# The last norm of a decoder step: sums of squares on TensorE block by block, the three column groups in another order, the last scaling on VectorE alone

## The chip, the core and the metric

The kernel runs on one core of a Trainium2 chip. The metric is the device time of one execution in microseconds. The profile shows one execution, with the engines PE (TensorE matmuls), PEld (TensorE weight loads), DVE (VectorE), ACT (ScalarE), POOL (GpSimd) and the DMA queues of SP and ACT.

## The reference

One layer of a hybrid autoregressive decoder is applied to 1024 prompt tokens and to 64 sampled tokens (8 sequences of 8). Each token has 1024 values. A token-mixing sub-layer (short convolution, dilated attention, sliding-window attention) and a SwiGLU feed-forward sub-layer add to the residual stream, each with its own modulated RMSNorm. At the end comes a plain RMSNorm, and it is this part that the change touches:

```
def rmsnorm(x, g):
    x32 = x.astype(jnp.float32)
    y = x32 * lax.rsqrt(jnp.mean(x32 * x32, axis=-1, keepdims=True) + EPS)
    return (y * g.astype(jnp.float32)).astype(x.dtype)

def swiglu(h, w_gate_up, w_down):
    gate, up = jnp.split(h @ w_gate_up, 2, axis=-1)
    return (jax.nn.silu(gate) * up) @ w_down
...
    x = x + gate2 * swiglu(rmsnorm(x, g_ffn) * (1 + scale2) + shift2, w_gate_up, w_down)
...
    y_prompt = rmsnorm(y_p, norm_final)
    y_sample = rmsnorm(y_s, norm_final)
```

## The kernel before

Everything is held transposed: a token is a column, its 1024 values lie in 8 blocks of 128 partitions. The residual stream is `x1[0]` to `x1[7]`, each 128 x 1088 in float32, columns 0 to 1023 the prompt and 1024 to 1087 the sampled tokens. All large matmuls are made in three passes (lines 204 to 206, `mm3`): weights and activations are each split into a high and a low half, and high x high, high x low and low x high are added up in PSUM. PSUM has eight banks, given out under four tags: `g` three, `s` two, `t` two, `o` one.

The feed-forward hidden values are made in groups of two blocks of 128 (`FF_GROUPS`); each group's down projection is added to the residual stream. For all groups but the last this goes by `down_all`. For the last group the columns are cut in three by `LAST`, so that the final norm of one group of columns can go on beside the down projection of the next. The last hidden block is split into its halves in three column parts (`split_hid`, lines 852 and 853): columns 366 to 731 first, 0 to 365 next, 732 to 1087 last.

For one group of n columns the code before does this:

1. For each of the 8 blocks m, `down` (line 1063): six matmuls of n columns into a bank with tag `g`, then `add_gated` on VectorE: bank times gate plus `x1[m]` (line 764), and for the sampled tokens two more short operations (768, 769).
2. `rstd` (line 1064): ScalarE squares each `x1[k]` (791, 794); seven adds gather the squares in `lacc` (795), on VectorE or GpSimd as `FADD` says; then, for each tile of 128 columns, a matmul with `lacc` as the stationary operand and a column of ones sums over the partitions (798). In the trace each tile shows as two passes.
3. `inv_rms` (lines 233 to 239): six short operations on VectorE and a square root on ScalarE give one scale per token.
4. The scale is spread over all partitions by matmuls with the identity (802) into a bank with tag `s`.
5. The scaling: for the blocks in `FPOOL` ScalarE multiplies with the gain (1071) and GpSimd with the scale (1072), which ScalarE has copied out of PSUM (1067); for the others VectorE does both in one operation (1074). Each block then goes out by its own DMA (1075), issued in turn by ScalarE and SyncE.

The program is written with a tile framework that orders each engine's instructions when it is built: it plays the program through with modelled durations and lets an engine take, of the instructions that are ready, the one that stands first in the code. So work that stands later in the code can be drawn ahead, but the engine then runs the order fixed at build time and waits wherever the chip is late. The pool `fin` takes the memory of the pool `sums`, whose last reader is a matmul of the last hidden block.

Of the kernel before, what the change touches and what calls it, by code (L numbers as in the profile page):

```python
# [8 lines left out]
F32 = mybir.dt.float32  # L9
F32R = mybir.dt.float32r  # L10
AF = mybir.ActivationFunctionType
OP = mybir.AluOpType
# [3 lines left out]
KC = 8  # L16
# [10 lines left out]
GRP = ((0, 366), (366, 366), (732, 356))  # L27
NB = 10
CONV_B = ((0,), (), (1,))
LAST = ((0, 416), (416, 416), (832, 256))  # L30
FF_GROUPS = ((0, 4), (20, 2)) + tuple((f, 2) for f in range(4, 20, 2))


# [12 lines left out]
ACCE = tuple("vvvvvggv")  # L46
MIXE = tuple("vgvgvgvg")
NADD = tuple("gggvgggv")
FADD = (tuple("ggvggvgv"), tuple("vgggvgvg"), tuple("vvvvvvvv"))
FPOOL = ((2, 3, 4), (1, 2, 3, 4, 5), (2, 4, 7))  # L50

MODN = (2, 1, 1, 0, 1, 0, 1, 1, 2, 1, 2, 0)
NPRE = 2
# [2 lines left out]
def build(nc, tc, d):  # L56
    st = tc.tile_pool
    with st(name="const", bufs=1) as cst, st(name="rows", bufs=1) as rows, \
            st(name="act", bufs=1) as actp, st(name="stream", bufs=1) as stream, \
            st(name="psum", bufs=1, space=PSUM) as psum:  # L60
        _build(nc, tc, d, cst, rows, actp, stream, psum)


def _build(nc, tc, d, cst, rows, actp, stream, psum):
    V, S, G, PE, SP = nc.vector, nc.scalar, nc.gpsimd, nc.tensor, nc.sync
# [3 lines left out]
    start = ExitStack()  # L69
    stp = start.enter_context(tc.tile_pool(name="start", bufs=1))  # L70

    def eng(c):
        return G if c == "g" else V

    def ps_tile(tag):
        bufs = {"g": PSB[0], "s": PSB[1], "t": PSB[2], "o": PSB[3]}[tag]
        return psum.tile([128, 512], F32, tag=tag, bufs=bufs, name="ps_" + tag)

    def row(name):
        return rows.tile([128, T], F32, tag="row", bufs=ROWS, name=name)  # L80
# [55 lines left out]
    gT = cst.tile([128, 24], F32, name="gT")  # L136
# [7 lines left out]
    ones = cst.tile([128, 1], F32, name="ones")  # L144
# [67 lines left out]
    def asel(acts, g):  # L212
        n = GRP[g][1] + (state["nb"] if acts is h and g == 2 else 0)
        return n, lambda h, k: acts[g][:, h, k, :n]
# [13 lines left out]
    def inv_rms(pool, sums, n):  # L228

        v = pool.tile([128, n], F32, tag="ir_v", bufs=2, name="ir_v")  # L230
        y = pool.tile([128, n], F32, tag="ir_y", bufs=2, name="ir_y")
        t = pool.tile([128, n], F32, tag="ir_t", bufs=2, name="ir_t")
        V.tensor_scalar(v, sums, 1.0 / D, EPS, op0=OP.mult, op1=OP.add)
        S.activation(y, v, AF.Sqrt)
        V.reciprocal(y, y)
        V.tensor_mul(t, y, y)
        V.tensor_mul(t, t, v)
        V.tensor_scalar(t, t, -0.5, 1.5, op0=OP.mult, op1=OP.add)
        V.tensor_mul(y, y, t)
        return y  # L240
# [11 lines left out]
    for item in "m0 w0 m1 x0 x1 m2 x2 m3 x3 x4 w1 x5 x7 x6 m4 m5 m6 m7".split():  # L252
        kind, i = item[0], int(item[1:])
# [37 lines left out]
    for k in range(KC):  # L291
        if k % 2 == 0:
            mod_tile(k // 2, bank="o" if k % 4 else "t")
        r, s = xr[k], MOD[:, 8 + k, 0:1]
        ts = stp.tile([128, NS], F32, tag="tsx", bufs=2, name="tsx")
        V.tensor_tensor(bi(ts), bi(r[:, SEQ:]), modb(8 + k), op=OP.mult)
        for g, (c0, n) in enumerate(GRP):
            m = min(n, SEQ - c0)
            S.activation(h[g][:, 0, k, :m], r[:, c0:c0 + m], AF.Copy, scale=s)
            V.scalar_tensor_tensor(h[g][:, 1, k, :m], r[:, c0:c0 + m], s, h[g][:, 0, k, :m].bitcast(F32),  # L300
                                   op0=OP.mult, op1=OP.subtract)
# [3 lines left out]
        for b in range(2):  # L305
            for g in range(3):
                n, a = asel(h, g)
# [68 lines left out]
    for i, (name, scale) in enumerate(early):  # L376
        r = prow[name] = row("p_" + name)
# [9 lines left out]
    c0 = GRP[2][1]  # L387
# [4 lines left out]
    for i, (name, scale) in enumerate(early):  # L392
        ps = ps_tile(SHB[i % 4])
        first = None
        for hf in range(2):
            for q in (3, 2, 1, 0):
                with tc.issue_after(first.ins) if first is not None else ExitStack():
                    ins = PE.matmul(ps[32 * q:32 * q + 32, :128], lhsT=shT[:, hf * 4 + q, :],
                                    rhs=wraw[i, hf][:, q * 128:q * 128 + 128], start=(hf == 0), stop=(hf == 1))
# [209 lines left out]
    mx, x1 = {}, {}  # L609
# [25 lines left out]
    ps = ps_tile("t")  # L635
# [138 lines left out]
    def tmp():  # L774
        if "ff" in scratch:
            return scratch["ff"].tile([128, 416], F32, tag="tmp", bufs=3, name="tmp")
        scratch["i"] = i = (scratch.get("i", 0) + 1) % 13
        return scratch["free"][:, 768 + 366 * i:768 + 366 * (i + 1)]
# [6 lines left out]
    def rstd(rng, adds, acc):  # L785

        c0, n = rng
        nt = (n + 127) // 128
        if n < nt * 128:
            G.memset(acc[:, n:nt * 128], 1.0)  # L790
        S.activation(acc[:, :n], x1[0][:, c0:c0 + n], AF.Square)
        for k in range(1, KC):
            sq = tmp()
            S.activation(sq[:, :n], x1[k][:, c0:c0 + n], AF.Square)
            eng(adds[k]).tensor_add(acc[:, :n], acc[:, :n], sq[:, :n])
        ps = ps_tile("t" if "ff" in scratch else "g")
        for t in range(nt):
            PE.matmul(ps[:, t:t + 1], lhsT=acc[:, t * 128:(t + 1) * 128], rhs=ones, start=True, stop=True)
        y = inv_rms(cst, ps[:, :nt], nt)
        r = ps_tile("s" if "ff" in scratch else "g")  # L800
        for t in range(nt):
            PE.matmul(r[:, t * 128:(t + 1) * 128], lhsT=y[:, t:t + 1].to_broadcast([128, 128]), rhs=ident,
                      start=True, stop=True)
        return r
# [3 lines left out]
    def second_rstd(g):  # L808
        return rstd(GRP[g], NADD, acc_tile(g))
# [45 lines left out]
    def down(w, m, rng, hid):  # L855
        c0, n = rng
        ps = ps_tile("g")
        mm3(ps, w, [(k, k) for k in range(len(hid))], lambda hl, k: hid[k][:, hl, c0:c0 + n], n)
        add_gated(m, rng, ps, 40)
# [69 lines left out]
    with tc.tile_pool(name="ffn", bufs=1, reuse_waits="tile") as ff:  # L929
# [96 lines left out]
        for f0, nf in FF_GROUPS[:1]:  # L1026
# [8 lines left out]
            for m in range(KC):  # L1035
                ps = ps_tile("g")
# [17 lines left out]
        fin = sums.enter_context(tc.tile_pool(name="fin", bufs=1, reuse_waits="tile"))  # L1054
# [3 lines left out]
        for q in range(4):  # L1058
            w = wsel(split(d["w_d2"][f0 // 2 - 2, q]))
            ws += [lambda hl, k, w=w, x=x: w(hl, 2 * x + k) for x in range(2)]  # L1060
        for g, (c0, n) in enumerate(LAST):
            for m in range(KC):
                down(ws[m], m, (c0, n), hid)
            r = rstd((c0, n), FADD[g], fin.tile([128, 512], F32, tag="lacc", bufs=1, name="lacc"))
            if FPOOL[g]:
                rs = fin.tile([128, 416], F32, tag="rs", bufs=1, name="rs")
                S.activation(rs[:, :n], r[:, :n], AF.Copy)
            for k in range(KC):
                y, gain = x1[k][:, c0:c0 + n], gT[:, 16 + k:17 + k]
                if k in FPOOL[g]:  # L1070
                    S.activation(y, y, AF.Copy, scale=gain)
                    G.tensor_tensor(y, y, rs[:, :n], op=OP.mult)
                else:
                    V.scalar_tensor_tensor(y, y, gain, r[:, :n], op0=OP.mult, op1=OP.mult)
                (SP if k % 2 else S).dma_start(d["yT"][k][:, c0:c0 + n], y)
        sums.close()
    assert not state["copies"]

# [140 lines left out]
```

## Time and profile before

| | us |
|---|---|
| median of 3 runs | 1404.19 |
| lowest and highest run | 1402.57, 1410.77 |
| the profiled execution | 1407.32 |
| its span in the profile | 1405.5 |
| mean granted clock of TensorE | 0.981 of full |
| VectorE busy | 839.7 |
| ScalarE busy | 582.6 |
| GpSimd busy | 329.6 |

The profiled execution was 1407.32 us by the device's time; its trace covers 1405.5 us of that. A row of the order of time gives the start, the duration, the engine, the line, the operation, what it writes and reads, and how often (xN) it stands in a row; in brackets is the time that the engine was idle before it, and whom it waited for. A row of a group gives the count, the busy time in us and the mean in ns of one, then the idle time before them. Matmuls overlap: the distance from one start to the next is what one costs in a stream, not its duration. A row of a table by stretch gives its bounds, its length, the busy time of each engine with the number of instructions, the granted clock, the share of the DMA engines and GB/s.

### The profile page before, as it was taken

The page shows a single profiled execution, that of the slowest core. Times are in us where ns is not written, and L with a number is a line of the kernel's source. Part 1 is how long each engine was busy: PE and PEld are TensorE (multiplying, and loading weights), DVE is VectorE, ACT ScalarE, POOL GpSimd, SP SyncE. Part 2 cuts the span into 40 slices and gives each one's busy share as a digit, 9 for nine tenths or more (in the row PEclk, how much of TensorE's full clock was granted, in tenths as well). Part 3 has the DMA queues.
Part 4 walks back from the last instruction along what each step waited for, and adds up shares of the span by engine and source line. Part 5 has one row for each costly group of instructions (what it writes and reads, how often), then busy time and mean ns, then how long its engine had stood idle before and what let it go on. Part 6 is the DMA issues. An engine that isn't in the chain of part 4 may idle for free.

```text
span 1405.5 us, 23915 instructions
## 1 busy us (share of the span) xinstructions
PE 1353.1 (96%) x9097; PEld 1288.3 (92%) x9097; DVE 839.7 (60%) x1935; ACT 582.6 (41%) x1204; POOL 329.6 (23%) x364
## 2 busy tenths in 40 slices
PE   7999999999999998899998999999999999999995
PEld 5889999988898887798998999999999999999994
DVE  5467768255676326224569675757565666665656
ACT  5397764365654335132345413141313232322243
POOL 2143343233424230102124020202111111111114
PEclk9999999999999999999999999999999999999996
DMA  9342431352416669675443413151515142323103
GB/s 356 113 160 99 135 99 24 129 197 91 144 24 218 216 240 362 239 284 174 112 134 93 143 38 120 30 180 31 188 30 187 51 160 81 137 83 128 44 30 128
DMA packets 77188, 190.91 MB, mean 136 GB/s; under 512 B 14048, under 2 KB 23808, under 8 KB 76288
## 3 DMA queue, kind: packets, MB, share of 16 engines
q1 hardware_dynamic: 73376, 135.67, 29.5%
q10 hardware_dynamic: 3536, 53.65, 10.6%
q8 instruction: 72, 1.18, 0.3%
q14 instruction: 44, 0.36, 0.1%
q0 software_dynamic: 160, 0.04, 0.0%
HBM read 181.32 MB, written 59.33 MB: 171 GB/s over the span
## 4 chain that ended last, share of the span: by engine, by line
PE 86%; DVE 6%; DMA 4%; issue 2%; ACT 1%; POOL 1%; POOLq 0%; SPq 0%; ACTq 0%; DVEq 0%
PE ps_g L204 19%; PE ps_g L205 19%; PE ps_g L206 19%; PE ps_s L205 3%; PE ps_s L204 3%; PE ps_s L206 3%; PE ps_o L578 2%; PE ps_t L205 2%; PE ps_t L204 2%; PE ps_t L206 2%; PE ps_t L569 2%; DMA wraw<-in_w_gu 1%; PE ps_g L179 1%; PE ps_s L527 1%; PE ps_s L528 1%
## 5 line engine op out<-in xcount | busy, mean ns | idle before, releaser
L204 PE MATMUL ps_g<-act,wsp 128*128 128x366 f32 (+1 forms) x1192 | 400.1, 337 | 2.6 <-DVE u L327 2.6
L206 PE MATMUL ps_g<-act,wsp 128*128 128x366 f32 (+1 forms) x1192 | 395.9, 333 | 4.0 <-DVE wsp L91 4.0
L205 PE MATMUL ps_g<-act,wsp 128*128 128x366 f32 (+1 forms) x1192 | 398.0, 334 | 0.5 <-DVE act L616 0.5
L90 ACT ACTIVATE wsp<-wraw 128x512 fp32r<-128x512 f32 x232 | 145.4, 629 | 278.1 <-PE ps_g L206 170.1
L204 PEld LDWEIGHTS ps_g<-act,wsp 128*128 128x128 f32 x1192 | 227.5, 191 | 9.9 <-issue 6.1
L206 PEld LDWEIGHTS ps_g<-act,wsp 128*128 128x128 f32 x1192 | 227.1, 191 | 8.3 <-DVE wsp L91 5.0
L205 PEld LDWEIGHTS ps_g<-act,wsp 128*128 128x128 f32 x1192 | 227.9, 191 | 4.3 <-issue 3.3
L91 DVE TENSOR_TENSOR wsp<-wraw,wsp 128x512 fp32r<-128x512 f32 x194 | 144.8, 747 | 145.1 <-ACT wsp L90 140.0
L204 PE MATMUL ps_g<-hid,wsp 128*128 128x366 f32 (+3 forms) x464 | 152.4, 331 | 5.0 <-DVE ts L768 3.6
L205 PE MATMUL ps_g<-hid,wsp 128*128 128x366 f32 (+3 forms) x464 | 152.4, 329 | 0.7 <-DVE hid L853 0.7
L206 PE MATMUL ps_g<-hid,wsp 128*128 128x366 f32 (+3 forms) x464 | 152.9, 330 | 0.0
L973 POOL TENSOR_TENSOR tw<-wraw 128x512 f32<-128x512 f32 x16 | 22.4, 1400 | 322.3 <-DMA wraw<-in_w_gu 244.3
L204 PEld LDWEIGHTS ps_g<-hid,wsp 128*128 128x128 f32 x464 | 87.8, 190 | 7.1 <-issue 3.6
L90 ACT ACTIVATE wsp<-tw 128x512 fp32r<-128x512 f32 x64 | 40.5, 633 | 122.5 <-PE ps_g L206 59.3
L204 PE MATMUL ps_s<-act,wsp 128*128 128x366 f32 x272 | 90.1, 331 | 0.0
L205 PE MATMUL ps_s<-act,wsp 128*128 128x366 f32 x272 | 90.0, 331 | 0.0
L206 PE MATMUL ps_s<-act,wsp 128*128 128x366 f32 x272 | 89.8, 330 | 0.0
L91 POOL TENSOR_TENSOR wsp<-wraw,wsp 128x512 fp32r<-128x512 f32 x38 | 49.9, 1312 | 169.2 <-ACT wsp L90 159.2
L205 PEld LDWEIGHTS ps_g<-hid,wsp 128*128 128x128 f32 x464 | 88.0, 190 | 1.1 <-DVE hid L853 1.0
L206 PEld LDWEIGHTS ps_g<-hid,wsp 128*128 128x128 f32 x464 | 88.1, 190 | 0.0
L764 DVE SCALAR_TENSOR_TENSOR p_qc<-ps_g,MOD,p_qc 128x366 f32<-128x366 f32 (+3 forms) x99 | 56.5, 572 | 39.4 <-PE ps_g L206 37.5
L764 DVE SCALAR_TENSOR_TENSOR p_q<-ps_g,MOD,p_q 128x366 f32<-128x366 f32 (+3 forms) x99 | 55.3, 569 | 38.4 <-PE ps_g L206 38.4
(346 smaller groups left out, 2454.7 us busy)
## 6 DMA issues: line engine op xcount, KB each, us to landing
wraw<-in_w_gu SPq DMA_DIRECT2D x112, 256.0 KB, 2.7
wraw<-in_wmod SPq DMA_DIRECT2D x64, 256.0 KB, 3.8
raw<-in_bk SPq DMA_DIRECT2D x30, 512.0 KB, 7.2
raw<-in_bv SPq DMA_DIRECT2D x30, 512.0 KB, 8.4
wraw<-in_w_in SPq DMA_DIRECT2D x36, 256.0 KB, 4.4
wraw<-in_w_d SPq DMA_DIRECT2D x36, 256.0 KB, 2.6
mraw<-in_wmod SPq DMA_DIRECT2D x32, 256.0 KB, 5.6
wraw<-in_w_out SPq DMA_DIRECT2D x32, 256.0 KB, 2.7
```

The costliest lines, as they stand in the source:

```text
L90: S.activation(sp[:, 0, :], raw, AF.Copy)
L91: (V if not state["sub"] or state["n"] % state["sub"] else G).tensor_tensor(sp[:, 1, :], raw, sp[:, 0, :].bitcast(F32), op=OP.subtract)
L179: ins = PE.matmul(ps[32 * q:32 * q + 32, :256], lhsT=csil[:, 4 * hf + q, :], rhs=raws[2 * hf + q // 2][:, q % 2 * 256:q % 2 * 256 + 256], ...
L204: PE.matmul(ps[:, :n], lhsT=w_hi, rhs=a(0, ak), start=first and j == 0, stop=False, **kw)
L205: PE.matmul(ps[:, :n], lhsT=w_hi, rhs=a(1, ak), start=False, stop=False, **kw)
L206: PE.matmul(ps[:, :n], lhsT=w_lo, rhs=a(0, ak), start=False, stop=last and j == m - 1, **kw)
L527: PE.matmul(ps[:, :sn], lhsT=QH[:, qsl], rhs=KS[hd][:, kk], start=True, stop=False)
L528: PE.matmul(ps[:, :sn], lhsT=QLO[:, qsl], rhs=KS[hd][:, kk], start=False, stop=True)
L569: PE.transpose(pt[:, col:col + 128], Sb[:, (kb - k0) * 128:(kb - k0 + 1) * 128], ident)
L578: PE.matmul(po[:, q0:q0 + w], lhsT=Vt[:, kb, hd].rearrange("p a b -> p (a b)"), rhs=PT[:, hl, c0:c0 + w], start=fresh, stop=ch is chunks[- ...
L764: ins = V.scalar_tensor_tensor(x1[m][:, c0:c0 + k], ps[:, :k], MOD[:, gate + m, 0:1], x1[m][:, c0:c0 + k], op0=OP.mult, op1=OP.add)
L973: G.tensor_tensor(t1, b12, b11, op=OP.subtract)
```

## The change

- `LAST` becomes (672 to 1087), (0 to 415), (416 to 671): the group that holds the sampled tokens is done first, and the last one has 256 columns of the prompt alone.
- The adds of `FADD` go. After each block's evacuation ScalarE squares it into one of four buffers `sq`, and a set of matmuls with ones adds that block's squares up in one PSUM bank `ss` (tag `t`), over all eight blocks. The buffers' columns from 384 on are set to one at the start, by GpSimd.
- `FPOOL`, the copy `rs` and GpSimd's part of the scaling go: all blocks are scaled on VectorE.
- Only the first four blocks of a group are scaled right after its scale is there; the other four are written behind the next group's norm, the last group's behind its own first four.
- `rstd` gives its spreading to a new function `spread`; its other callers do the same work as before.

```
-LAST = ((0, 416), (416, 416), (832, 256))
+LAST = ((672, 416), (0, 416), (416, 256))
...
-FADD = (tuple("ggvggvgv"), tuple("vgggvgvg"), tuple("vvvvvvvv"))
-FPOOL = ((2, 3, 4), (1, 2, 3, 4, 5), (2, 4, 7))
...
-        y = inv_rms(cst, ps[:, :nt], nt)
+        return spread(inv_rms(cst, ps[:, :nt], nt), nt)
+
+    def spread(y, nt):
+
         r = ps_tile("s" if "ff" in scratch else "g")
         for t in range(nt):
             PE.matmul(r[:, t * 128:(t + 1) * 128], lhsT=y[:, t:t + 1].to_broadcast([128, 128]), rhs=ident,
...
-        for g, (c0, n) in enumerate(LAST):
+        sqs = [fin.tile([128, 512], F32, name=f"sq{i}") for i in range(4)]
+        for sq in sqs:
+            G.memset(sq[:, 384:], 1.0)
+
+        def scale_out(rng, r, ks):
+            c0, n = rng
+            for k in ks:
+                y = x1[k][:, c0:c0 + n]
+                V.scalar_tensor_tensor(y, y, gT[:, 16 + k:17 + k], r[:, :n], op0=OP.mult, op1=OP.mult)
+                (SP if k % 2 else S).dma_start(d["yT"][k][:, c0:c0 + n], y)
+
+        late = None
+        for c0, n in LAST:
+
+            nt = (n + 127) // 128
+            ss = ps_tile("t")
             for m in range(KC):
                 down(ws[m], m, (c0, n), hid)
-            r = rstd((c0, n), FADD[g], fin.tile([128, 512], F32, tag="lacc", bufs=1, name="lacc"))
-            if FPOOL[g]:
-                rs = fin.tile([128, 416], F32, tag="rs", bufs=1, name="rs")
-                S.activation(rs[:, :n], r[:, :n], AF.Copy)
-            for k in range(KC):
-                y, gain = x1[k][:, c0:c0 + n], gT[:, 16 + k:17 + k]
-                if k in FPOOL[g]:
-                    S.activation(y, y, AF.Copy, scale=gain)
-                    G.tensor_tensor(y, y, rs[:, :n], op=OP.mult)
-                else:
-                    V.scalar_tensor_tensor(y, y, gain, r[:, :n], op0=OP.mult, op1=OP.mult)
-                (SP if k % 2 else S).dma_start(d["yT"][k][:, c0:c0 + n], y)
+                sq = sqs[m % 4]
+                S.activation(sq[:, :n], x1[m][:, c0:c0 + n], AF.Square)
+                for t in range(nt):
+                    PE.matmul(ss[:, t:t + 1], lhsT=sq[:, t * 128:(t + 1) * 128], rhs=ones, start=(m + t == 0),
+                              stop=(m == KC - 1 and t == nt - 1))
+            r = spread(inv_rms(cst, ss[:, :nt], nt), nt)
+            if late:
+                scale_out(*late, range(4, KC))
+            scale_out((c0, n), r, range(4))
+            late = ((c0, n), r)
+        scale_out(*late, range(4, KC))
```

## The prediction

> **What bounds the kernel now.** I read the page's head first, then a table by stretch of the last 50 us, where every edited line lies, then the order of time of each engine in it.
>
> ```profile
> span 1405.5 us, 23915 instructions
> PE 1353.1 (96%) x9097; PEld 1288.3 (92%) x9097; DVE 839.7 (60%) x1935; ACT 582.6 (41%) x1204; POOL 329.6 (23%) x364
> ```
>
> ```profile
> core 0: us, PE busy (x) PEld busy (x) DVE busy (x) ACT busy (x) POOL busy (x), PEclk, DMA share, GB/s
> 1355.30:1364.20 8.90, 8.90 (x49) 8.89 (x49) 7.03 (x13) 6.13 (x12) 3.27 (x3) 1.00 0.01 2
> ...
> 1377.90:1381.60 3.70, 0.25 (x3) 0.07 (x2) 3.70 (x9) 0.00 (x0) 3.00 (x4) 1.00 0.59 221
> 1381.60:1387.90 6.30, 6.30 (x32) 6.11 (x32) 4.98 (x23) 3.28 (x9) 0.86 (x1) 0.57 0.39 143
> 1387.90:1397.20 9.30, 2.82 (x13) 2.63 (x12) 7.06 (x19) 2.06 (x5) 5.14 (x5) 0.50 0.42 145
> 1397.20:1405.50 8.30, 1.22 (x4) 0.93 (x4) 2.05 (x5) 0.38 (x1) 2.10 (x3) 0.50 0.50 171
> ```
>
> The whole program is bound by TensorE, busy 96% of the span, and the tail begins the same way: in the first row PE is full, and its weight loads with it; the rows left out up to 1377.9 look the same. Then come two losses. From 1377.9 to 1381.6 PE stands while VectorE is full, and its clock is granted at 0.57 and 0.50 from there on. After 1387.9, when the last down projection is done, 17.6 us remain in which PE has little to do. These rows tell what stands there:
>
> ```profile
> 1381.58 0.36 PE L204 MATMUL ps_g<-hid,wsp 128*128 128x256 f32 x1 [3.45 <-DVE ts L768]
> 1387.59 0.41 PE L206 MATMUL ps_g<-hid,wsp 128*128 128x256 f32 x1
> 1397.24 1.22 PE L802 MATMUL ps_s<-ident,ir_y 128*128 128x128 f32 x4 [5.40 <-DVE ir_y L239]
> 1398.58 0.38 ACT L1067 ACTIVATE rs<-ps_s 128x256 f32<-128x256 f32 x1 [4.73 <-PE ps_s L802]
> 1399.00 0.87 DVE L1074 SCALAR_TENSOR_TENSOR cv<-cv,gT,ps_s 128x256 f32<-128x256 f32 x2 [1.81 <-ACT rs L1067]
> 1400.18 0.87 DVE L1074 SCALAR_TENSOR_TENSOR p_qc<-p_qc,gT,ps_s 128x256 f32<-128x256 f32 x2
> ```
>
> The last scale factor is spread at 1397.24 to 1398.46, the last scaling of VectorE ends at 1401.05, and the span ends 4.4 us later, after the output's transfers. So the end is set by one string: down projections and whatever PE does between them, the last group's norm, its scaling, its transfers.
>
> **The change part by part.** I lay the new tail out from the same start, 1355.30, since PE is full ahead of it and nothing before it is edited.
>
> The down projections stay, in another order.
>
> ```profile
> 1355.30 0.35 PE L204 MATMUL ps_g<-hid,wsp 128*128 128x416 f32 x1
> 1364.26 0.36 PE L204 MATMUL ps_g<-hid,wsp 128*128 128x416 f32 x1
> ...
> 1375.93 0.28 PE L205 MATMUL ps_g<-hid,wsp 128*128 128x256 f32 x1
> 1377.85 0.28 PE L206 MATMUL ps_g<-hid,wsp 128*128 128x256 f32 x1
> ```
>
> Eight blocks of six matmuls over 416 columns take 8.96 us (0.187 each); over 256 columns sixteen starts take 1.92, so 0.12 each and 5.76 for eight blocks. Sum 8.96 + 8.96 + 5.76 = 23.7 us at full clock.
>
> The new first group ends at column 1088, so it reads the last third of the hidden tile, which the old first group did not.
>
> ```profile
> 1355.54 0.52 DVE L1020 TENSOR_TENSOR u<-u,ps_g 128x356 f32<-128x356 f32 x1
> 1356.82 0.52 DVE L853 TENSOR_TENSOR hid<-u,hid 128x356 fp32r<-128x356 f32 x1
> ```
>
> A product, a high half between the two on ScalarE, and the low half at 1357.34. The halves of the other hidden tile are there, and the blocks that have a bank (three for these outputs) can do their first three matmuls: 9 x 0.187 = 1.7 us of work against 2.04 us. I take 0.5 us of waiting; the ends are 0 and 1.5 (one block's three matmuls alone as cover).
>
> The sums of squares are the large term. Before, twelve VectorE and nine GpSimd adds gathered the eight squares and one set of small matmuls summed over partitions per group; now every block has its own set. What a set costs in the stream of PE shows twice:
>
> ```profile
> 1368.63 0.35 PE L206 MATMUL ps_g<-hid,wsp 128*128 128x416 f32 x1
> 1368.82 0.95 PE L798 MATMUL ps_t<-ones,lacc 128*128 128x1 f32 x8
> 1369.91 0.35 PE L205 MATMUL ps_g<-hid,wsp 128*128 128x416 f32 x1
> ```
>
> ```profile
> 713.02 0.33 PE L204 MATMUL ps_g<-act,wsp 128*128 128x366 f32 x1
> 713.19 0.72 PE L798 MATMUL ps_t<-ones,acc 128*128 128x1 f32 x6
> 714.02 0.33 PE L206 MATMUL ps_g<-act,wsp 128*128 128x366 f32 x1
> ```
>
> L206 to the next block's L205 takes 1.28 where two steps of 0.187 would do: 0.90 us for four tiles. In the second case L204 to L206 takes 1.00 where two steps of 0.167 would do: 0.67 for three. So 0.22 a tile, two passes each. New: 8 x (4 + 4 + 2) = 80 tiles, 18.0 us, of which the last group's last two sets come after its last down projection. Gone are three sets at the ends of the groups.
>
> The additions and the GpSimd half of the scaling go; VectorE takes all of the scaling.
>
> ```profile
> L795 POOL TENSOR_TENSOR lacc<-lacc,tmp 128x416 f32<-128x416 f32 x9 | 9.8, 1088 | 17.6 <-ACT tmp L794 13.5 <-DVE lacc L795 3.0 <-ACT lacc L791 0.8
> L764 DVE SCALAR_TENSOR_TENSOR p_q<-ps_g,MOD,p_q 128x416 f32<-128x416 f32 x6 | 3.9, 651 | 2.8 <-PE ps_g L206 2.8
> L794 ACT ACTIVATE tmp<-p_q 128x416 f32<-128x416 f32 x6 | 3.3, 545 | 0.4 <-DVE p_q L764 0.4
> L795 DVE TENSOR_TENSOR lacc<-lacc,tmp 128x256 f32<-128x256 f32 x7 | 2.9, 420 | 0.5 <-ACT ir_y L234 0.4
> L1074 DVE SCALAR_TENSOR_TENSOR p_qc<-p_qc,gT,ps_s 128x416 f32<-128x416 f32 x5 | 2.9, 637 | 0.0
> L795 DVE TENSOR_TENSOR lacc<-lacc,tmp 128x416 f32<-128x416 f32 x5 | 2.9, 580 | 0.0
> L1074 DVE SCALAR_TENSOR_TENSOR cv<-cv,gT,ps_s 128x256 f32<-128x256 f32 x2 | 0.9, 478 | 1.8 <-ACT rs L1067 1.8
> ```
>
> VectorE loses 2.9 + 2.9 us of adds and gains 8 x 0.637 + 3 x 0.478 = 6.5 us: even. Against PE's new step of 6 x 0.187 + 0.90 = 2.02 us a block it needs 0.65 for the evacuation (two short ones more where the sampled tokens are) and ScalarE 0.55 for the square, so both stay off the bound, and what they wait for is PE. GpSimd drops out; its memsets of 128 columns are done before the first square. The 24 output transfers stay; twelve are issued from ScalarE's queue, where each waits for its scaling with the next squares behind it, and PE's next sums behind those.
>
> That matters where scalings come in a burst. A group's first four scalings are written ahead of the next group's evacuations: 4 x 0.637 = 2.6 us. In the second group three banks of 1.12 us cover it; in the third, three of 0.72 = 2.2 us do not quite. I take 0.5 us of PE standing, with ends 0 and 3 (all eight in one burst, 5.1 - 2.2). The other four have late places and no hurry; VectorE should fill its gaps with them, and I let one of them (0.64) and its seam stand in the last norm's way: 0.8, ends 0 and 2.6.
>
> The end of the string becomes shorter. The copy of the scale (L1067, 0.38 and a VectorE that waits for it) goes, and with GpSimd idle the small operations should run as in the first two groups:
>
> ```profile
> L237 DVE TENSOR_TENSOR ir_t<-ir_t,ir_v 128x2 f32<-128x2 f32 x1 | 1.0, 983 | 0.0
> L237 DVE TENSOR_TENSOR ir_t<-ir_t,ir_v 128x4 f32<-128x4 f32 x2 | 0.3, 158 | 0.0
> ```
>
> The slow one ran while GpSimd scaled. Six such operations at 0.16 and a root at 0.2 on ScalarE make 1.3 us with their seams.
>
> The sum: 1355.30 + 0.5 start + 23.7 + 16 x 0.90 + 6 x 0.45 sums + 2 x 0.9 for the first two groups' spreading (taken as eight passes, like a set of sums) + 0.5 burst = 1398.9 for the last down projection (1388.0 before). Then evacuation, square and seams 1.25, the last set and its drain 0.65, the norm 1.3 + 0.8, spreading two tiles at full clock 0.65 (half of the 1.22 above) and a seam 0.15: scaling starts at 1403.7. Eight scalings at 0.41 (five took 2.05 us from 1399.00) end at 1407.0, and 4.0 us to the end, a little under the 4.4 of before since the transfers are spread: 1411.0. Against 1405.5 that is **+5.5 us**. The profiled execution took 1407.32 us, 1.8 around its span, unchanged; the median of the three runs shown is 1404.19, and I put the same step on it: 1409.7.
>
> PE's stream grows by 11 us, and the shorter end gives back about half. With the ends of the unknowns (start -0.5 to +1.0, burst -0.5 to +2.5, late scaling -0.8 to +1.8, end -0.5 to +0.4) the likeliest case spans +3 to +11: 1407 to 1415.
>
> **The clock, and a rule on it.** The granted clock decides whether the 18 us of sums stay 18. It fell once more in this trace with PE hardly idle:
>
> ```profile
> 529.00:531.00 2.00, 0.81 (x12) 0.34 (x16) 1.10 (x5) 1.20 (x1) 0.00 (x0) 1.00 1.10 374
> 531.00:533.00 2.00, 1.17 (x16) 0.19 (x8) 0.34 (x2) 0.00 (x0) 0.41 (x2) 0.90 1.07 405
> 533.00:535.00 2.00, 2.00 (x13) 1.86 (x9) 0.68 (x3) 1.22 (x1) 0.41 (x2) 0.50 1.01 414
> ```
>
> PE was half busy for four microseconds, in short pieces, and the clock went to 0.50. The Trainium skill, page "TensorE: Matmul & The Clock Gate", section "Part 1: The HAM clock gate", puts the fall after an idle window of about 3.4 us; by it alone no fall comes here and the sum stands. Its section "A second HAM failure mode: psum-queue depth-cycling" says that frequent short idling between groups of matmuls makes the clock swing; this trace's stretch at 529 looks like that, and the result is the first rival.
>
> **The rivals.**
> - Slower: the clock falls among the sums. In each 2.02 us only 1.12 us stream columns, and passes of one column may not count as work. At 0.50 a block of the third group takes about twice its 0.72 + 0.45, so +9.4 us for that group: 1419. It is over 1% slower from nine more microseconds than the sum on, that is, with about 9 us of the full-clock work done at half. Against it: the one set at 1368.82 was passed without a fall, the next matmuls keeping their 0.35. 0.12.
> - Slower: the sums stand in PE's queue before their squares are done. Evacuation 0.65, square 0.55 and three seams need 1.5 us, with sampled tokens 1.9; the next block's matmuls give 1.12. Where the written order has nothing else between, PE waits 0.4 to 0.8 at 24 sets, about 14 us with all of them: 1424. Against it: the order is planned with such delays in it, and neither set quoted above, at 713.19 and 1368.82, has an idle time in front. 0.10.
> - Faster than forecast: the one-column passes hide, as loads under the 416-column matmuls. With one pass of two hidden, 9 us go: 1401, no change to before. Against it: the loads are busy 8.89 of 8.90 us already. 0.10.
>
> **How the numbers follow.** The forecast has 0.68, the rivals 0.12, 0.10 and 0.10. The runs of before spread from 1402.57 to 1410.77, so about 1% is what tells a change from none here; that is 14 us, over a quarter of the edited tail. Faster by 1% would need the tail cut to 36 us, which PE's 23.7 + 18.0 alone exceed: 0.01. Slower by 1% (from 1418.2) takes over half of the two slower rivals and a little of the forecast: 0.14. Same: 0.85. The range goes from 1402, which leaves out part of the hidden passes, to 1419, which takes in the clock falling for one group.
>
> **What would show it.** Right: about 160 passes of one column between the down projections at 0.1 us, the last down projection ending near 1399, clock 1.00 there, small operations of the last norm at 0.16, scaling from about 1404. Wrong: PE idle before sums for a square; a clock of 0.5 before the last norm; VectorE's late scalings behind the last norm; or sets that cost well under 0.9 us.

## The result, and the profile after

| | before | after |
|---|---|---|
| median of 6 runs, us | 1406.55 | 1422.03 |
| lowest and highest run | 1402.57, 1410.77 | 1420.59, 1432.23 |
| the profiled execution | 1407.32 | 1421.83 |
| first down projection of the tail | 1355.30 | 1357.31 |
| from there to the end of the last one | 32.7 | 47.7 |
| from there to the end of the span | 17.5 | 14.9 |

The changed kernel is **slower by 1.3%**: ratio 1.0131, interval 1.0099 to 1.0162. Forecast was 1409.7 us. Two executions of kernels below, one of spaced_sums and one of late_behind, were in a slower state and are left out of the ratios, which compare the executions and not the medians beside them.

Apart from the memsets of the new buffers on GpSimd, each engine's order is the same in both programs up to the first down projection of the last hidden group, so the 2.0 us by which this tail begins later are spread between executions (in the kernels below it begins between 1349.4 and 1361.7). The tail itself grew from 50.2 to 62.6 us; the forecast was 43.6 and 12.1, together 55.7. So 4.1 us are missing from the forecast before the end of the last down projection, and 2.8 behind it.

The head of the page of the profile after:

```profile
span 1419.9 us, 24162 instructions
PE 1370.6 (97%) x9237; PEld 1304.9 (92%) x9237; DVE 837.7 (59%) x1934; ACT 575.6 (41%) x1190; POOL 309.1 (22%) x346
```

PE has 17.5 us more, VectorE 2 less. The tail by stretch, after (columns as in the prediction):

```profile
core 0: us, PE busy (x) PEld busy (x) DVE busy (x) ACT busy (x) POOL busy (x), PEclk, DMA share, GB/s
1357.30:1366.30 9.00, 8.85 (x51) 8.44 (x50) 6.99 (x22) 3.58 (x7) 0.00 (x0) 1.00 0.01 2
1366.30:1370.10 3.80, 3.80 (x35) 3.80 (x34) 0.00 (x0) 0.55 (x1) 0.00 (x0) 1.00 0.00 0
1370.10:1377.00 6.90, 6.90 (x25) 6.65 (x25) 2.53 (x7) 1.24 (x3) 0.00 (x0) 0.51 0.00 0
1377.00:1394.80 17.80, 17.77 (x130) 17.38 (x129) 10.74 (x23) 6.48 (x12) 0.00 (x0) 1.00 0.28 97
1394.80:1397.40 2.60, 2.60 (x26) 2.60 (x25) 0.89 (x4) 0.62 (x2) 0.00 (x0) 1.00 0.00 0
1397.40:1400.90 3.50, 3.50 (x19) 3.50 (x19) 1.07 (x5) 0.42 (x1) 0.00 (x0) 0.52 0.02 5
...
1405.00:1410.40 5.40, 2.47 (x12) 2.30 (x12) 3.33 (x7) 1.22 (x3) 0.00 (x0) 0.76 0.68 254
1410.40:1419.90 9.50, 1.19 (x4) 0.93 (x4) 4.20 (x14) 0.20 (x1) 0.00 (x0) 0.50 0.34 112
```

PE is shown full almost without a break from 1366.3 to 1400.9, and yet its clock is granted at 0.51 for 6.9 us and at 0.52 for 3.5. Up to half of these 10.4 us, some 5, is lost. The row ahead of each of them holds little but matmuls of one column, as the order of time of PE in the same trace shows:

```profile
1366.36 3.63 PE L1083 MATMUL ps_t<-ones,sq 128*128 128x1 f32 x32
1372.41 0.55 PE L204 MATMUL ps_g<-hid,wsp 128*128 128x416 f32 x1
...
1377.36 0.35 PE L204 MATMUL ps_g<-hid,wsp 128*128 128x416 f32 x1
1377.55 0.95 PE L1083 MATMUL ps_t<-ones,sq 128*128 128x1 f32 x8
1378.63 0.35 PE L203 MATMUL ps_g<-hid,wsp 128*128 128x416 f32 x1
...
1394.81 2.73 PE L1083 MATMUL ps_t<-ones,sq 128*128 128x1 f32 x24
...
1404.71 0.28 PE L204 MATMUL ps_g<-hid,wsp 128*128 128x256 f32 x1
1405.87 0.61 PE L1083 MATMUL ps_t<-ones,sq 128*128 128x1 f32 x4 [0.88 <-ACT sq L1081]
1408.50 1.87 PE L1083 MATMUL ps_t<-ones,sq 128*128 128x1 f32 x8 [2.02 <-ACT sq L1081]
```

The order fixed at build time put four sets of the first group together (x32, 3.63 us) and later two sets of the second and two of the last (x24, 2.73 us; a set is eight passes at 416 columns and four at 256). Within 4 us of each start the clock falls, and behind the first run a matmul of 416 columns shows 0.55 (1372.41) where it shows 0.35 at full clock (1377.36). A set that stands by itself (1377.55) costs what was forecast: 1.27 from the start of L204 to that of L203, less two steps of 0.187, is 0.90.

Behind the last down projection PE waits twice for a square, 0.88 and 2.02 us, and the last two sets (x8, 1.87 us) run at half clock. VectorE's order of time, after, says what made the squares late:

```profile
1402.59 1.21 DVE L1070 SCALAR_TENSOR_TENSOR cv<-cv,gT,ps_s 128x416 f32<-128x416 f32 x2 [1.00 <-PE ps_s L803]
...
1405.22 0.64 DVE L1070 SCALAR_TENSOR_TENSOR p_q<-p_q,gT,ps_s 128x416 f32<-128x416 f32 x1
1405.78 1.76 DVE L1070 SCALAR_TENSOR_TENSOR p_qc<-p_qc,gT,ps_s 128x416 f32<-128x416 f32 x3
1407.45 0.87 DVE L762 SCALAR_TENSOR_TENSOR p_qc<-ps_g,MOD,p_qc 128x256 f32<-128x256 f32 x2
1410.40 0.16 DVE L231 TENSOR_SCALAR ir_v<-ps_t 128x2 f32<-128x2 f32 x1 [2.08 <-PE ps_t L1083]
1411.23 0.16 DVE L235 TENSOR_TENSOR ir_t<-ir_t,ir_v 128x2 f32<-128x2 f32 x1
```

As soon as the second group's scale is there, at 1402.59, all eight of its scalings (L1070) are done in a burst that reaches to 1407.5, with one evacuation between them; the last two evacuations (L762) stand behind it at 1407.45, two and a half microseconds after their matmuls. "Four now, four later" is an order of the code only: the planner drew the later four ahead as well.

### The profile page after: what moved, and what is told of

It is laid out like the page before. It is cut to its first block, busy times and chain, and to the rows that moved or that the text cites. A ratio compares the mean times of both kernels' runs of the same rounds, so it can differ in the third digit from the quotient of the medians.

```text
span 1419.9 us, 24162 instructions
## 1 busy us (share of the span) xinstructions
PE 1370.6 (97%) x9237; PEld 1304.9 (92%) x9237; DVE 837.7 (59%) x1934; ACT 575.6 (41%) x1190; POOL 309.1 (22%) x346
## 3 DMA queue, kind: packets, MB, share of 16 engines
q10 hardware_dynamic: 3536, 53.65, 10.4%
## 4 chain that ended last, share of the span: by engine, by line
PE 89%; DVE 5%; DMA 3%; issue 1%; ACT 1%; POOL 1%; SPq 0%; DVEq 0%; ACTq 0%; POOLq 0%
PE ps_g L202 20%; PE ps_g L203 19%; PE ps_g L204 19%; PE ps_s L203 3%; PE ps_s L202 3%; PE ps_s L204 3%; PE ps_o L576 2%; PE ps_t L203 2%; PE ps_t L202 2%; PE ps_t L204 2%; PE ps_t L567 2%; PE ps_g L177 1%; PE ps_s L525 1%; PE ps_t L1083 1%; PE ps_s L526 1%
## 5 line engine op out<-in xcount | busy, mean ns | idle before, releaser
L204 PE MATMUL ps_g<-act,wsp 128*128 128x366 f32 (+1 forms) x1192 | 395.6, 333 | 4.0 <-DVE wsp L89 4.0
L203 PE MATMUL ps_g<-act,wsp 128*128 128x366 f32 (+1 forms) x1192 | 398.0, 334 | 0.5 <-DVE act L614 0.5
L204 PEld LDWEIGHTS ps_g<-act,wsp 128*128 128x128 f32 x1192 | 227.2, 191 | 8.2 <-DVE wsp L89 5.0
L203 PEld LDWEIGHTS ps_g<-act,wsp 128*128 128x128 f32 x1192 | 227.9, 191 | 4.3 <-issue 3.3
L203 PE MATMUL ps_g<-hid,wsp 128*128 128x366 f32 (+3 forms) x464 | 153.4, 331 | 1.5 <-DVE hid L854 1.4
L204 PE MATMUL ps_g<-hid,wsp 128*128 128x366 f32 (+3 forms) x464 | 153.9, 332 | 0.0
L203 PEld LDWEIGHTS ps_g<-hid,wsp 128*128 128x128 f32 x464 | 88.7, 191 | 2.4 <-DVE hid L854 2.1
L203 PE MATMUL ps_s<-act,wsp 128*128 128x366 f32 x272 | 90.2, 332 | 0.0
L204 PE MATMUL ps_s<-act,wsp 128*128 128x366 f32 x272 | 90.0, 331 | 0.0
L204 PEld LDWEIGHTS ps_g<-hid,wsp 128*128 128x128 f32 x464 | 88.5, 191 | 0.1
L762 DVE SCALAR_TENSOR_TENSOR p_qc<-ps_g,MOD,p_qc 128x366 f32<-128x366 f32 (+4 forms) x99 | 56.3, 572 | 46.2 <-PE ps_g L204 44.2
L762 DVE SCALAR_TENSOR_TENSOR p_q<-ps_g,MOD,p_q 128x366 f32<-128x366 f32 (+4 forms) x99 | 55.3, 570 | 42.2 <-PE ps_g L204 42.1
```

The costliest lines, as they stand in the source:

```text
L203: PE.matmul(ps[:, :n], lhsT=w_hi, rhs=a(1, ak), start=False, stop=False, **kw)
L204: PE.matmul(ps[:, :n], lhsT=w_lo, rhs=a(0, ak), start=False, stop=last and j == m - 1, **kw)
L762: ins = V.scalar_tensor_tensor(x1[m][:, c0:c0 + k], ps[:, :k], MOD[:, gate + m, 0:1], x1[m][:, c0:c0 + k], op0=OP.mult, op1=OP.add)
```

## The experiments

Two theories stood at the start. **Clock**: passes of one column don't keep TensorE's clock (in the expectations A, where long runs of them count, and B, where their share counts). **Burst**: the late scalings make the last squares late (C). Rivals were that the loss lies in the number of passes, in VectorE taking over the scaling, or in the order of the groups. The tails in us, each from its one profiled execution, which can lie several us beside its kernel's median (late_behind 1412.62 for 1422.04, wide_ones 1421.55 for 1416.03, spaced_sums 1444.84 for 1438.57):

| kernel | to the end of the last down | from there to the end | ratio to before, interval |
|---|---|---|---|
| before | 32.7 | 17.5 | 1 |
| after | 47.7 | 14.9 | 1.0131 (1.0099 to 1.0162) |
| spaced_sums | 74.6 | 13.8 | 1.0188 (1.0117 to 1.0259) |
| wide_ones | 43.4 | 14.4 | 1.0068 (1.0045 to 1.0091) |
| spaced_wide | 46.2 | 14.3 | 1.0062 (1.0037 to 1.0087) |
| late_behind | 46.3 | 12.9 | 1.0093 (1.0061 to 1.0124) |
| wide_late | 43.1 | 12.2 | 1.0021 (1.0000 to 1.0042) |
| f32r_wide_late | 34.1 | 15.4 | 0.9975 (0.9948 to 1.0002) |
| f32r_norm_first_pool | 34.2 | 15.6 | 0.9997 (0.9974 to 1.0021) |
| ones_first | 32.5 | 19.2 | 1.0011 (0.9989 to 1.0033) |
| before_dve_scale | 33.6 | 17.6 | 1.0007 (0.9983 to 1.0032) |
| before_norm_first | 33.6 | 17.7 | 1.0005 (0.9979 to 1.0030) |
| before_last_order | 29.2 | 21.5 | 1.0006 (0.9974 to 1.0038) |

**spaced_sums**: the same sums, but each block's set is tied into PE's order behind the down projection two blocks later, so that no two sets stand together until the last three.

```
+                    with tc.issue_after(state["mm"].ins):   # the last matmul of the down projection just written
+                        b = todo.pop(0)                     # the block two before
+                        behind = sum_set(*b)                # the next down projection is issued after it
```

> The changed kernel with PE's order fixed: each block's set of sums stands right behind the down projection two blocks later, so no two sets stand together until the last three. Theory A (the clock falls because long runs of one-column passes, 3.6 us at 1366.4 and 2.7 us at 1394.8, count as idle): 1.00 is granted through all the down projections, the last one ends about 5 us earlier counted from the first (47.7 us in the changed kernel, so near 42.5), the time is near 1417. Theory B (the clock falls because 45% of the time goes to one-column passes, wherever they stand): the clock falls as often, the time stays near 1422. Theory C (the late scalings ahead of the last evacuations are the main loss, the clock a minor one): within 2 us of 1422.

It came out the slowest by its median, 1438.57 us, but its four executions spread from 1424.35 to 1447.11 and its ratio is not clear of that of after. The trace is of one of the long ones, 1444.84. Order of time of PE in spaced_sums, and two stretches of its tail:

```profile
1359.94 1.82 PE L1087 MATMUL ps_t<-ones,sq 128*128 128x1 f32 x8 [1.95 <-ACT sq L1105]
...
1363.86 1.70 PE L1087 MATMUL ps_t<-ones,sq 128*128 128x1 f32 x8
```

```profile
1358.00:1362.00 4.00, 2.06 (x9) 2.06 (x10) 1.74 (x8) 1.43 (x3) 0.00 (x0) 0.75 0.02 4
1362.00:1424.00 62.00, 62.00 (x243) 60.74 (x243) 18.28 (x47) 10.50 (x20) 0.00 (x0) 0.50 0.08 28
```

The fixed order made the first set wait 1.95 us for its square; the clock fell there, and then it stayed at 0.50 for 62 us in which PE is shown busy 62.00 of 62.00. So "a long run of one-column passes" was too narrow: spaced sets don't bring a fall by themselves, as the 17.8 us at 1.00 in after show (single sets of 0.95 between the down projections, and one pair of 1.84), but once the clock is down, sets that take 1.70 of each 3.8 us seem to keep it down. Whether that is the columns or the fixed order with its wait, spaced_wide below tells.

**wide_ones**: the ones become a matrix of 128 columns, so that each pass streams 128 columns instead of one; the loads and the number of passes stay, and the order is planned anew.

```
-                    PE.matmul(ss[:, t:t + 1], lhsT=sq[...], rhs=ones, ...)
+                    PE.matmul(ss[:, t * 128:(t + 1) * 128], lhsT=sq[...], rhs=ones_w, ...)
```

> The changed kernel with 128 columns of ones in place of one: the same number of passes and the same loads, 0.90 us for a set of four tiles as with the spreading (also 128 columns), but columns stream through the array all the time. Theory A in the form that idle columns are what counts: the clock stays at 1.00 until the last down projection, which ends near 42.5 us from the first, time near 1417. If it is the passes' loads or gaps that count and not the columns: falls as in the changed kernel, 1422. If a set costs more with 128 columns: the last down projection ends later than 47.7 us at a clock of 1.00.

PE's order of time and the table by stretch of wide_ones:

```profile
1370.70 3.73 PE L1085 MATMUL ps_t<-ones_w,sq 128*128 128x128 f32 x32
...
1396.39 2.85 PE L1085 MATMUL ps_t<-ones_w,sq 128*128 128x128 f32 x24
```

```profile
1370.70:1374.40 3.70, 3.70 (x34) 3.70 (x34) 0.00 (x0) 0.55 (x1) 0.00 (x0) 1.00 0.00 0
1374.40:1396.40 22.00, 21.60 (x155) 21.33 (x154) 13.20 (x30) 7.73 (x14) 0.00 (x0) 1.00 0.22 79
```

The same runs of 32 and 24 passes, at the same price (3.73 and 2.85 us), and the clock holds 1.00 behind the first where it fell in after. PE's order is the same as in after past the first run, and differs by some matmuls later. So the columns per pass are what the clock went by there; 47.7 becomes 43.4, what the forecast had for full clock (43.6), and the interval of the ratio lies clear of that of after.

**spaced_wide**: both edits together.

> The kernel with the sets of sums spaced out in PE's fixed order (which ran at half clock for 60 us), with 128 columns of ones in place of one. If the missing columns kept the clock down there: 1.00 through the down projections, the last one ends 44 to 46 us from the first (2 us of waiting for the first square stay), time 1412 to 1418, against 1438. If it was the fixed order with its wait: half clock again, over 1425.

```profile
1364.07 1.13 PE L1089 MATMUL ps_t<-ones_w,sq 128*128 128x128 f32 x8 [2.04 <-ACT sq L1107]
```

```profile
1362.46:1371.00 8.54, 6.93 (x38) 6.89 (x39) 3.20 (x13) 1.98 (x4) 0.00 (x0) 0.80 0.01 2
1371.00:1404.60 33.60, 33.60 (x256) 33.44 (x255) 19.13 (x48) 10.82 (x21) 0.00 (x0) 1.00 0.17 60
```

Its first set waits 2.04 us, as in spaced_sums (first fence, order of time), and the clock dips to a mean of 0.80 (second, by stretch); but here it comes back and stays at 1.00 for 33.6 us. One-column passes thus do both: they let the clock fall when they stand together, and they keep it from returning when they stand often.

The granted clock of the traces has a pattern behind this. In each of the thirteen, the moments at which it changes lie 3.41 us or a multiple of that apart (in after 1370.23, 1377.06, 1397.54, 1400.95 and 1407.78). I divided every tail into such windows and added up the time in which matmuls of more than one column run, an estimate, since their ends are modelled. A full clock fell behind 17 windows, all with about 1.6 us of such work or less, and held behind 122 with about 1.6 or more; a halved one came back behind five with 2.71 or more, and stayed behind 27 with 2.47 or less. Ahead of the falls at 1370.23 and 1397.54 it is 0.27 and 0.82 us, the rest of the 3.41 going to one-column passes.

The Trainium skill, page "TensorE: Matmul & The Clock Gate", section "Part 1: The HAM clock gate", puts the fall after an idle window of about 3.4 us and the return after as long a busy one. The traces agree on the length, if one-column passes count as idle, which that section does not say; but a window need not be all idle, since the clock of spaced_wide fell behind a wait of 2.04 us. The section "A second HAM failure mode: psum-queue depth-cycling" of that page speaks of micro-idling between groups of matmuls. PE shows no such idling in after: it is busy 34.56 of the 34.60 us from 1366.3 to 1400.9.

**late_behind**: the four later scalings may be issued only behind the last evacuation of the group that follows.

```
+                ev = down(ws[m], m, (c0, n), hid)
...
             if late:
-                scale_out(*late, range(4, KC))
+                with tc.issue_after(ev.ins):
+                    scale_out(*late, range(4, KC))
```

> The changed kernel, with a group's four late scalings issued on VectorE behind the next group's last evacuation. Theory C (a burst of eight scalings holds the last two evacuations of the last group, about 3.5 us): from the last down projection to the end 11.5 us in place of 14.9, the time near 1418.5. Theory A (the clock): the falls stay where they are, the time stays within 1.5 us of 1422 unless the last sums come sooner too.

PE's order of time in late_behind:

```profile
1397.45 0.28 PE L204 MATMUL ps_g<-hid,wsp 128*128 128x256 f32 x1
1399.43 0.61 PE L1083 MATMUL ps_t<-ones,sq 128*128 128x1 f32 x4 [1.36 <-ACT sq L1081]
```

The end shrank from 14.9 to 12.9 us. The last down projection starts its last matmul at 1397.45 and the first late set stands at 1399.43, with one wait of 1.36 us in front of it where after has two, together 2.90. The order planned anew has no second long run of sums, and in this trace the clock falls only once ahead of the end of the down projections. By itself, against after, the gain in the ratio (1.0131 to 1.0093) is not clear, and the median, 1422.04 us, is that of after; on top of wide ones it is, just:

**wide_late**: wide_ones and late_behind together, which brings the change near to what the forecast assumed.

> Both single edits on the changed kernel: 128 columns of ones, and the late scalings behind the next group's last evacuation. If the two causes are separate they add: the last down projection ends 43.4 us from the first, 12.9 us from there to the end, a tail of 56.2 us and 6 us over before: near 1412, the forecast's own sum. If the clock alone explains it: 1416 as with the 128 columns alone.

The tail of wide_late by stretch, cut at the end of the last down projection:

```profile
1357.52:1400.66 43.14, 42.99 (x313) 42.30 (x312) 25.59 (x67) 13.85 (x27) 0.00 (x0) 1.00 0.15 51
1400.66:1412.90 12.24, 2.35 (x13) 1.88 (x12) 6.82 (x19) 1.04 (x3) 0.00 (x0) 0.68 0.54 190
```

43.1 and 12.2 us, where the prediction's sum has 43.6 and 12.1. The time is 1411.14 us median, ratio 1.0021; against before it is no longer over 1%. In ratios the loss of 1.31% so divides into 0.63 for the clock (after to wide_ones), 0.47 for the burst (wide_ones to wide_late) and 0.21 for what is left; with intervals of 0.2 to 0.3 on each these are sizes, not digits. In the tails of the single executions the same steps are 4.8, 2.4 and 5.1 us.

**f32r_wide_late**: squares and ones held as F32R, which PE takes in one pass a tile (80 passes for 160).

```
-        sqs = [fin.tile([128, 512], F32, name=f"sq{i}") for i in range(4)]
+        sqs = [fin.tile([128, 512], F32R, name=f"sq{i}") for i in range(4)]
```

> As with both edits, and the squares and the ones in the format that the large matmuls use, so that a tile's sum is one pass and not two (the squares are rounded a little more). If the passes' own time on PE is what is left of the loss: 9 us less on PE, the last down projection ends near 35 us from the first, a tail near 47.5 and a time 3 us under before, 1403. If VectorE sets the pace once PE is relieved: less than half of the 9 us shows.

By stretch, then VectorE's order of time in it:

```profile
1349.50:1383.60 34.10, 33.30 (x228) 32.74 (x227) 22.77 (x63) 14.02 (x28) 0.00 (x0) 1.00 0.15 51
1383.60:1399.00 15.40, 2.95 (x21) 2.54 (x19) 9.15 (x23) 0.74 (x3) 0.00 (x0) 0.70 0.51 180
```

```profile
1384.78 1.21 DVE L1072 SCALAR_TENSOR_TENSOR cv<-cv,gT,ps_s 128x416 f32<-128x416 f32 x2 [0.63 <-PE ps_s L803]
...
1389.25 0.15 DVE L231 TENSOR_SCALAR ir_v<-ps_t 128x2 f32<-128x2 f32 x1
...
1393.96 1.26 DVE L1072 SCALAR_TENSOR_TENSOR p_qc<-p_qc,gT,ps_s 128x256 f32<-128x256 f32 x3
```

PE's part falls by 9.0 us, half the 18 of sums; the end grows by 3.2. Now VectorE is late: the second group's scalings begin at 1384.78, and the last norm's first operation stands behind them at 1389.25. This is the best version, 1404.45 us, ratio 0.9975 (0.9948 to 1.0002): not clear of before.

**f32r_norm_first_pool**: the last norm ahead of those scalings but one, and three of them (k 5 to 7) given to ScalarE and GpSimd.

```
+                    for k in POOL_K:                        # 5, 6, 7
+                        S.activation(y, y, AF.Copy, scale=gT[:, 16 + k:17 + k])
+                        go = G.tensor_tensor(y, y, rs[:, :pn], op=OP.mult)
...
+                with tc.issue_after(state["rms"].ins):      # the last norm's last operation
+                    scale_out(*late, [k for k in range(1, KC) if k not in POOL_K])
```

> On top of the one-pass sums over 128 columns: of the second group's scalings only one may stand in front of the last norm, four come behind its small operations on VectorE, and three go to ScalarE (gain) and GpSimd (scale). If VectorE's burst of eight in front of the last norm is what kept its end at 15.4 us after the last down projection: the norm starts 3 to 4 us sooner, VectorE has 1.9 us less to do, the end comes near 13 us after the last down projection, a tail near 47: 1401 to 1402, clear of before. If the output's transfers (2.75 MB after the second group's scale is there) set the end: no more than 1 us better than the one-pass sums alone, 1404.

VectorE's order of time, GpSimd's, and a stretch of the end:

```profile
1386.47 0.16 DVE L235 TENSOR_TENSOR ir_t<-ir_t,ir_v 128x2 f32<-128x2 f32 x1
...
1387.64 0.97 DVE L237 TENSOR_TENSOR ir_y<-ir_y,ir_t 128x2 f32<-128x2 f32 x1
...
1392.73 1.25 DVE L1072 SCALAR_TENSOR_TENSOR p_qc<-p_qc,gT,ps_s 128x256 f32<-128x256 f32 x3
```

```profile
1386.52 3.10 POOL L1102 TENSOR_TENSOR p_qc<-p_qc,rs 128x416 f32<-128x416 f32 x3 [44.03 <-ACT rs L1098]
```

```profile
1391.00:1396.00 5.00, 0.00 (x0) 0.00 (x0) 2.98 (x8) 0.00 (x0) 0.00 (x0) 0.50 1.03 361
```

The norm now ends at 1388.6, but the time did not move (0.9997). GpSimd works from 1386.52 on, and a 128x2 operation then takes 0.97 us instead of 0.16. And the outputs of two groups now go out together: from 1391 to 1396 the DMA engines are full (share 1.03) with 361 GB/s, where f32r_wide_late, whose tail begins 0.1 us later, has 0.52 and 170 in the same stretch. Over their whole ends both move about the same, 176 and 180 GB/s. VectorE's last scaling ends 1.2 us sooner (1393.98 for 1395.22), and the span does not end sooner (1399.3 for 1399.0). I read the transfers as the next limit; no run took them away, so that is argued, not shown.

**ones_first**: ones as the stationary operand and the squares streamed (as F32R, with the late scalings held back as above), which gives the sum in every partition and needs no spreading, but makes the norm's operations as wide as the group.

```
+                PE.matmul(ss[:, :n], lhsT=ones_w, rhs=sq[:, :n], start=(m == 0), stop=(m == KC - 1))
+            r = inv_rms(fin, ss[:, :n], n)
```

> As with both edits, but the ones are the stationary operand and a block's squares stream by in one pass (0.19 us a block where a set cost 0.90), so every partition gets the sums and the spreading falls away, while the norm's six small operations become operations over the group's columns (0.4 to 0.6 each on VectorE in place of 0.16). PE: 23.7 + 4.2 us. If PE's passes were the loss: the last down projection ends near 29 us. VectorE's work grows by about 8 us to 40, so it should set the pace: a tail of 46 to 50, near before, 1402 to 1406.

By stretch, and VectorE's order of time:

```profile
1389.54:1408.60 19.06, 1.16 (x6) 0.55 (x4) 15.54 (x29) 1.25 (x3) 0.00 (x0) 0.59 0.41 145
```

```profile
1388.53 2.74 DVE L233 RECIPROCAL ir_y<-ir_y 128x416 f32<-128x416 f32 x1
```

PE is done with the down projections after 32.5 us, as early as in before (32.7); VectorE then fills 15.54 of the last 19.06, a reciprocal over 416 columns taking 2.74 alone. No gain: 1.0011.

**The other parts alone, on the kernel before.** before_dve_scale replaces only the scaling (all on VectorE, four and four); before_norm_first also puts the second group's behind the last norm; before_last_order changes only the order of the groups.

```
-            if FPOOL[g]:
...
+            if late:
+                scale_out(*late, range(4, KC))
+            scale_out((c0, n), r, range(4))
+            late = ((c0, n), r)
```

> The kernel before, with only the scaling changed: all of it on VectorE, four blocks early and four late, without the copy of the scale; sums by adds, old group order. By the prediction's step on the end of the string (norm's small operations at 0.16 in place of up to 0.99, no copy): 3 to 4 us less than before, near 1402. Rival: eight scalings in a burst on VectorE hold evacuations and adds, and eat the gain: within 1.5 us of before, or over it.

> The kernel before with all scaling on VectorE, which gained nothing, but with the second group's scalings issued behind the last norm's small operations. If the gain of the shorter end was lost to that burst (the norm's second operation waited from 1396.3 to 1399.0): the norm ends 2 to 3 us sooner; but eight scalings then stand between it and the last group's, so the time gains 0.5 to 1.5 us if VectorE's work sets the end, 3 if the order alone does.

```
-LAST = ((0, 416), (416, 416), (832, 256))
+LAST = ((672, 416), (0, 416), (416, 256))
```

> The kernel before with the new order of the column groups alone: the group with the sampled tokens first of the three. By the prediction's step: up to 0.5 us of waiting at the start for the last third of the hidden values, and 16 short operations fewer beside the last group's evacuations; within 2 us of before. If the order is a cause of the loss: over 3 us slower.

VectorE's order of time in before_dve_scale, then in before_norm_first, then before_last_order by stretch:

```profile
1395.65 1.20 DVE L1066 SCALAR_TENSOR_TENSOR cv<-cv,gT,ps_s 128x416 f32<-128x416 f32 x2 [1.19 <-PE ps_s L802]
...
1399.01 0.15 DVE L233 TENSOR_SCALAR ir_v<-ps_t 128x2 f32<-128x2 f32 x1
```

```profile
1391.11 0.16 DVE L239 TENSOR_TENSOR ir_y<-ir_y,ir_t 128x2 f32<-128x2 f32 x1
1391.19 1.20 DVE L1066 SCALAR_TENSOR_TENSOR cv<-cv,gT,ps_s 128x416 f32<-128x416 f32 x2
...
1397.61 1.25 DVE L1066 SCALAR_TENSOR_TENSOR p_qc<-p_qc,gT,ps_s 128x256 f32<-128x256 f32 x3
```

```profile
1356.64:1385.80 29.16, 26.72 (x162) 25.47 (x160) 24.00 (x59) 16.36 (x31) 13.04 (x13) 1.00 0.14 49
1385.80:1407.30 21.50, 5.00 (x25) 4.53 (x24) 10.96 (x28) 5.07 (x14) 7.66 (x9) 0.56 0.40 144
```

None of the three moves the time: 1.0007, 1.0005, 1.0006. In the first the burst is back, six scalings from 1395.65 to the norm's first operation at 1399.01. In the second the norm is early (1391.27), but sixteen scalings follow in one piece, from 1391.19 to 1398.86. In the third the down projections end 3.5 us sooner and the end takes 4.0 more. So on the kernel before neither VectorE's scaling nor the order of the groups costs or brings anything clear of the intervals of about 0.3%. That leaves the sums; they were not put alone on the kernel before.

## Why the prediction was wrong

**The step that failed** is the paragraph on the clock, and the chance of 0.12 for the rival built on it. The sum took the down projections and the sums at full clock, 43.6 us; measured were 47.7, and 43.4 with 128 columns per pass. The mechanism that the rival names, "passes of one column may not count as work", is what happened; its place was the third group, and the falls came in the second and third. What spoke against it was one set of eight passes that was passed without a fall. That was poor evidence: 0.95 us among wide matmuls says nothing of 3.63 us in one piece, and I had priced the sums as if the sets would stand evenly spaced. Nothing in the trace of before could say so, since it has no two sets together; but that the order is fixed at build time from what is ready is told in the kernel's description, and that sets waiting for their squares may then stand together could have been worked out from it. The stretch at 529, called hardly idle, did not bear on it: PE was busy for 1.98 of its 4.00 us.

**The late scalings** were the second wrong step: "VectorE should fill its gaps with them", with 0.5 us for a burst and 0.8 for a scaling in the last norm's way. The end "all eight in one burst" was named, as the far end of a range, and it was the case, in both groups that have a successor. PE's waits of 0.88 and 2.02 us, and the last two sets at half clock, follow from it. With the burst held back the end is 12.2 us for 12.1; with it 14.4 (wide ones) or 14.9.

**Right** were the other terms. The start cost little: 8.85 of 9.00 us busy, against 0.5 forecast. A set costs 0.90 us. The sum at full clock is 43.1 to 43.4 us for 43.6. The last norm's small operations take 0.16 each without GpSimd. Of the rivals, waiting for the squares came to 2.9 us in after, not 14, and to 1.36 in late_behind without the burst; and the passes did not hide: halving their number, at 128 columns, took 9.0 us off PE's part, all that 18 of sums would give.

The tail is 6.9 us over the forecast (62.6 for 55.7), some 4 to 5 of it from the clock. What the range left out is that the burst's cost came on top of the clock's, as each case was priced with the other absent. The rest of the 12.3 us by which the median missed lies outside the tail: this execution's tail began 2.0 later, and 3.1 come from putting the step, worked out on an execution of 1407.32 us, on a median of 1404.19. Over six runs that median is 1406.55; from there the same sum gives 1412.1, still 10 us short.

## What to carry to other kernels

Full occupancy in the profile does not say that the clock is kept: look at how many columns each pass streams, and where passes of one column pile up or recur, give them more columns, which cost next to nothing here (3.73 us for 3.63). A step written "later" in the code is later only if something ties it there; before counting on it, look at what becomes ready at once and which engine takes it first. And when a bound is cut by 9 us, ask at once what is late next: here VectorE, and behind it probably the output's transfers, gave back about a third.

## What I had not expected of the hardware

A pass costs the same with one moving column and with 128 (3.63 and 3.73 us for 32 passes), but only the latter holds the granted clock; with one-column sets taking 1.70 of every 3.8 us the clock stayed at 0.50 for 62 us of uninterrupted work. One and the same mix leaves a full clock full and a halved one halved: single sets of 0.95 us and a pair of 1.84 were passed without a fall in 17.8 us of after, while 2.73 and 3.63 us in one piece were followed by one. In windows of 3.41 us the fall came at about 1.6 us of wider matmuls or less, the return at 2.71 or more. The slow 128x2 operations of the last norm go with GpSimd's work: in f32r_norm_first_pool 0.97 us beside it, and 0.16 for those begun before it.
